# Output projection of a hybrid attention layer: residual added in mid-product, two sums of y kept in DRAM, last product by token blocks

## The chip, the cores and the metric

The kernel runs on one core of a Trainium2 chip. The metric is the device time of one execution in microseconds (us). A core has a matrix engine (TensorE, PE in the profile, with its weight loads as PEld), a vector engine (VectorE, DVE), a scalar engine (ScalarE, ACT), a general engine (GpSimd, POOL) and SyncE (SP), whose queue issues every DMA of this kernel in program order.

## What is computed

One layer over 1024 tokens of width 2048: an input projection, sliding-window attention and gated linear attention on its pieces, an output projection, and a LayerNorm over the residual sum. The change touches only the end:

```python
y = jnp.einsum('bse,ed->bsd', jnp.concatenate([y_a, y_g], axis=-1), w_out[l])
x = _layer_norm(DN_ALPHA * x + y, ln_g[l], ln_b[l])      # mean and variance over 2048 columns
```

`y` going in is 1024 x 2048, `w_out` 2048 x 2048, everything float32.

## The kernel before

Up to about 1110 us the input projection and both attention groups run; their results, the input of the output projection, are stored transposed in DRAM (`yd`, sixteen 128-row pieces for each half H of the tokens). What follows is the stretch that matters here.

**Seven products.** Token half, inner half and column half make a 2 x 2 block product, done in Winograd's form with seven half-size products instead of eight, in the order 1, 6, 7, 4, 5, 3, 2. Sums of weight blocks were stored earlier in `td`; sums of `y` blocks are made on POOL when they are needed (`y_part`, L709 to L717): one subtraction for product 7, one addition for 5, two operations for 6, three for 3. A product has two column halves `fp` of 512, four blocks `t` of 128 tokens and eight steps `k` of 128 rows. float32 is split in a rounded part and a remainder (`split`, L109: ScalarE rounds, L113; VectorE subtracts, L114), and each step takes three matmuls 128 x 512 (L740 to L742): 96 for a column half, 192 for a product, 1344 in all.

**Loops.** For six products and the first half of the seventh, `k` is the outer loop and the four token blocks the inner one, in four PSUM banks; all four are complete together. In the second half of product 2 (`last`) the token block is the outer loop, so the blocks end one after another. When a bank is complete, `collect` adds it into the output rows `pre` (eight tiles 128 x 2048; blocks 0 to 3 are the upper token half, 4 to 7 the lower). The lower half is complete after product 5, the upper one after product 2.

**Residual, statistics, norm.** For columns 0 to 1023 the residual x is loaded into `pre` itself and scaled when a product is added. For columns 1024 to 2047 `residual(tb)` (L768) loads 512 KB into a slot of the pool `raw`, adds it on VectorE (L772) and takes two statistics; it runs after the second half of product 5 (lower half) and of product 3 (upper half). `norm` (L744) then works on 608 columns with ScalarE and POOL (L751 to L757) and on 1440 with VectorE (L761, L762), in three pieces of 480 for the very last block, and stores the rows.

**Slots and queues.** `raw` has four slots of 128 x 1024; weight loads (L728, L731) and residual loads share them. `wsp` holds eight split weight pieces, `xsp` sixteen split `y` pieces (a `y` sum's operands take slots there too). A scheduler orders each engine's instructions when the kernel is built, so an instruction can stand far from its place in the text; after that every engine and SyncE's queue keep their order, and what stands behind a waiting instruction waits too.

## Time and profile before

| | |
|---|---|
| runs | 1463.07, 1466.36, 1465.85 us, median 1465.85 |
| profiled execution | 1466.27 us, of which the profile's span is 1464.4 us |
| TensorE busy | 1419.3 us (97% of the span) |
| VectorE, ScalarE, POOL busy | 886.2, 605.9, 370.4 us (61%, 41%, 25%) |
| mean granted TensorE clock | 0.987 of full speed |
| HBM read, written | 184.66 MB, 33.55 MB |

Busy time is the union of an engine's instructions. Matmuls are pipelined: one takes about 0.39 us from its start to its end but the next starts earlier, so the rate is read from starts, and a busy TensorE says only that it did not wait. Times inside the span count from its start.

### The profile page before, as it was taken

How to read it: one execution, taken by the hardware profiler on the slowest of the kernel's cores; microseconds unless marked ns; L12 is line 12 of the kernel's file. 1: busy time of each engine (PE TensorE's matmuls, PEld its weight loads, DVE VectorE, ACT ScalarE, POOL GpSimd, SP SyncE). 2: the span in 40 equal slices, each digit the busy share in tenths (PEclk: the TensorE clock that was granted, in tenths of full speed). 3: DMA queues.
4: the chain of work that ended last, by engine and by line, in shares of the span. 5: the costliest groups of instructions: out<-in, count | busy, mean ns of one | idle time of the engine just before them, and what ended most of it. 6: DMA issues, size and time to landing. Idle time of an engine off the chain costs nothing.

```text
span 1464.4 us, 23613 instructions
## 1 busy us (share of the span) xinstructions
PE 1419.3 (97%) x8992; PEld 1183.5 (81%) x8992; DVE 886.2 (61%) x1522; ACT 605.9 (41%) x1278; POOL 370.4 (25%) x373
## 2 busy tenths in 40 slices
PE   8999999999999999999999999999999999997984
PEld 5888788888888977888889888888988888885763
DVE  5566556555655665566556555655565555567968
ACT  5544345434434554444335435443553434322321
POOL 0132211212221122232211221310023231465505
PEclk9999999999999999999999999999999999998987
DMA  8243344343434346443344343433235967666642
GB/s 311 94 150 113 126 131 145 120 132 127 148 109 137 117 158 214 138 138 123 122 145 137 123 132 119 148 108 115 94 113 179 360 204 222 192 217 210 215 130 115
DMA packets 101392, 224.47 MB, mean 153 GB/s; under 512 B 11040, under 2 KB 44192, under 8 KB 101024
## 3 DMA queue, kind: packets, MB, share of 16 engines
q1 hardware_dynamic: 101280, 222.98, 46.0%
q8 instruction: 70, 1.15, 0.3%
q14 instruction: 42, 0.34, 0.1%
HBM read 184.66 MB, written 33.55 MB: 149 GB/s over the span
## 4 chain that ended last, share of the span: by engine, by line
PE 92%; DVE 5%; DMA 1%; issue 1%; POOL 1%; ACT 0%; SPq 0%; DVEq 0%; ACTq 0%
PE acc L172 17%; PE acc L174 17%; PE acc L173 17%; PE acco L740 6%; PE acco L741 6%; PE acco L742 6%; PE accv L186 4%; PE accv L188 4%; PE accv L187 4%; PE po L291 2%; PE pa L360 1%; PE ps L260 1%; PE ps L259 1%; PE pt L281 1%; PE lracc L310 1%; DVE pre L762 1%
## 5 line engine op out<-in xcount | busy, mean ns | idle before, releaser
L114 DVE TENSOR_TENSOR wl<-raw,wh 128x512 fp32r<-128x512 f32 x445 | 344.4, 781 | 270.2 <-ACT wh L113 245.6
L113 ACT CAST wh<-raw 128x512 fp32r<-128x512 f32 x445 | 272.2, 620 | 444.5 <-PE acc L173 279.6
L172 PE MATMUL acc<-xh,wh 128*128 128x512 f32 x1088 | 429.4, 396 | 6.6 <-ACT wh L113 6.6
L174 PE MATMUL acc<-xh,wl 128*128 128x512 f32 x1088 | 426.6, 392 | 0.0
L173 PE MATMUL acc<-xl,wh 128*128 128x512 f32 x1088 | 426.5, 392 | 0.0
L172 PEld LDWEIGHTS acc<-xh,wh 128*128 128x128 f32 x1088 | 204.7, 188 | 53.8 <-ACT wh L113 7.6
L174 PEld LDWEIGHTS acc<-xh,wl 128*128 128x128 f32 x1088 | 204.6, 188 | 44.7 <-issue 1.4
L173 PEld LDWEIGHTS acc<-xl,wh 128*128 128x128 f32 x1088 | 204.8, 188 | 43.0 <-issue 2.2
L740 PE MATMUL acco<-wh,xh 128*128 128x512 f32 x436 | 168.0, 395 | 14.6 <-ACT wh L113 14.6
L741 PE MATMUL acco<-wl,xh 128*128 128x512 f32 x436 | 171.8, 394 | 3.9 <-DVE wl L114 3.9
L742 PE MATMUL acco<-wh,xl 128*128 128x512 f32 x436 | 171.0, 393 | 0.0
L186 PE MATMUL accv<-wh,xh 128*128 128x256 f32 x512 | 145.3, 284 | 0.0
L188 PE MATMUL accv<-wh,xl 128*128 128x256 f32 x512 | 145.0, 283 | 0.0
L187 PE MATMUL accv<-wl,xh 128*128 128x256 f32 x512 | 144.8, 283 | 0.0
L716 POOL TENSOR_TENSOR yr<-yr 128x512 f32<-128x512 f32 x56 | 79.6, 1424 | 150.1 <-DMA yr<-yd 145.3
L740 PEld LDWEIGHTS acco<-wh,xh 128*128 128x128 f32 x436 | 82.7, 190 | 32.7 <-ACT wh L113 15.5
L741 PEld LDWEIGHTS acco<-wl,xh 128*128 128x128 f32 x436 | 82.9, 190 | 22.0 <-DVE wl L114 4.6
L186 PEld LDWEIGHTS accv<-wh,xh 128*128 128x128 f32 x512 | 98.1, 192 | 1.2 <-issue 0.7
L188 PEld LDWEIGHTS accv<-wh,xl 128*128 128x128 f32 x512 | 98.1, 192 | 0.6 <-issue 0.3
L187 PEld LDWEIGHTS accv<-wl,xh 128*128 128x128 f32 x512 | 98.2, 192 | 0.5
L742 PEld LDWEIGHTS acco<-wh,xl 128*128 128x128 f32 x436 | 83.0, 190 | 17.3
L278 POOL TENSOR_TENSOR s<-s,sm 128x512 f32<-128x512 f32 x32 | 37.2, 1163 | 214.0 <-DVE sm L277 111.5
(173 smaller groups left out, 1707.2 us busy)
## 6 DMA issues: line engine op xcount, KB each, us to landing
raw<-in_w_e_dram SPq DMA_DIRECT2D x134, 512.0 KB, 3.9
yr<-yd SPq DMA_DIRECT2D x112, 256.0 KB, 4.8
raw<-in_w_v_dram SPq DMA_DIRECT2D x32, 512.0 KB, 4.4
raw<-in_w_out_dram SPq DMA_DIRECT2D x128, 128.0 KB, 2.6
td<-raw SPq DMA_DIRECT2D x32, 512.0 KB, 3.5
raw<-td SPq DMA_DIRECT2D x32, 512.0 KB, 4.3
raw<-in_w_out_dram SPq DMA_DIRECT2D x24, 512.0 KB, 4.5
raw<-in_xT_dram SPq DMA_DIRECT2D x15, 512.0 KB, 4.7
```

Source lines behind the costliest of these rows:

```text
L113: A.copy(hi, src)
L114: V.tensor_tensor(lo, src, hi.bitcast(F32), ALU.subtract)
L172: PE.matmul(acc, wh[:, c], xh, start=(k == 0), stop=False)
L173: PE.matmul(acc, wh[:, c], xl, start=False, stop=False)
L174: PE.matmul(acc, wl[:, c], xh, start=False, stop=(k == KT - 1))
L186: PE.matmul(o, xh[:, t], wh[:, c], start=(k == 0 and tb % 2 == 0), stop=False, skip_group_check=True)
L187: PE.matmul(o, xh[:, t], wl[:, c], start=False, stop=False, skip_group_check=True)
L188: PE.matmul(o, xl[:, t], wh[:, c], start=False, stop=(k == KT - 1), skip_group_check=True)
L716: G.tensor_tensor(a, a, b, ALU.add if sign > 0 else ALU.subtract)
L740: PE.matmul(acc, yh[:, c], wh, start=(k == 0), stop=False)
L741: PE.matmul(acc, yh[:, c], wl, start=False, stop=False)
L742: PE.matmul(acc, yl[:, c], wh, start=False, stop=(k == 7))
```

## The change

Four things. The residual of columns 1024 to 2047 gets two slots of its own (`res`) in place of the six slots that `last` used, and is loaded and added at the head of products 4 (upper half) and 5 (lower half); the statistics of those columns are taken by `collect` once a column half is complete. Product 6 stores two of its sums of `y` in DRAM (`ysum`, sixteen pieces of 256 KB), and products 5 and 3 load them: product 5 makes no sum any more, product 3 one instead of three. Product 2 takes the token block as its outer loop for both column halves, with the weights of the first half in slots of `xsp`.

```diff
@@ -159,6 +159,7 @@
 
 
     td = [dr_p.tile([P, 16, 4, 256], F32, name=f"td{f}") for f in range(2)]
+    ys_d = [dr_p.tile([P, 8 * T], F32, name=f"ysum{i}") for i in range(2)]
     yd = [[dr_p.tile([P, 4 * T], F32, name=f"yd{H}_{q}") for q in range(4)] for H in range(2)]
 
 
@@ -690,7 +691,7 @@
 
     op = ctx.enter_context(tc.tile_pool(name="op", bufs=5, space=PSUM, reuse_waits="tile"))
     lp = ctx.enter_context(tc.tile_pool(name="lp", bufs=1, reuse_waits="tile"))
-    w2_p = ctx.enter_context(tc.tile_pool(name="w2", bufs=3, reuse_waits="tile"))
+    r_p = ctx.enter_context(tc.tile_pool(name="res", bufs=2, reuse_waits="tile"))
     pre = [lp.tile([P, D], F32, name=f"pre{tb}") for tb in range(2 * NB)]
     stats = [lp.tile([P, 4, 6], F32, name=f"stats{tb}") for tb in range(2 * NB)]
     gb = lp.tile([P, D], F32, name="gb")
@@ -708,15 +709,30 @@
 
     def y_part(i, k):
 
-        at = {1: "00", 2: "01", 3: "01", 4: "11", 5: "10", 6: "10", 7: "00"}[i]
-        a = y_raw(int(at[0]), int(at[1]), k, "xh")
-        more = {3: ((0, 0, 1), (1, 0, -1), (1, 1, -1)), 5: ((1, 1, 1),), 6: ((1, 1, 1), (0, 0, -1)), 7: ((1, 0, -1),)}
-        for n, (h, g, sign) in enumerate(more.get(i, ())):
-            b = y_raw(h, g, k, "xl" if n % 2 == 0 else "xh")
-            G.tensor_tensor(a, a, b, ALU.add if sign > 0 else ALU.subtract)
+        at = {1: "00", 2: "01", 3: "01", 4: "11", 6: "10", 7: "00"}
+        if i == 5:
+            a = x_p.tile([P, T], F32, name="yr", tag="xh")
+            SP.dma_start(a, ys_d[0][:, k * T:k * T + T])
+            return split(a, x_p, "x")
+        a = y_raw(int(at[i][0]), int(at[i][1]), k, "xh")
+        if i == 6:
+            b = y_raw(1, 1, k, "xl")
+            c = y_raw(0, 0, k, "xl")
+            G.tensor_tensor(a, a, b, ALU.add)
+            SP.dma_start(ys_d[0][:, k * T:k * T + T], a)
+            G.tensor_tensor(c, a, c, ALU.subtract)
+            SP.dma_start(ys_d[1][:, k * T:k * T + T], c)
+            a = c
+        elif i == 7:
+            b = y_raw(1, 0, k, "xl")
+            G.tensor_tensor(a, a, b, ALU.subtract)
+        elif i == 3:
+            b = x_p.tile([P, T], F32, name="yr", tag="xl")
+            SP.dma_start(b, ys_d[1][:, k * T:k * T + T])
+            G.tensor_tensor(a, a, b, ALU.subtract)
         return split(a, x_p, "x")
 
-    def w_parts(i, fp, pools):
+    def w_parts(i, fp, pool, tag):
 
         out = []
         for q in range(4):
@@ -730,7 +746,6 @@
                     j = {5: 0, 7: 1, 4: 2, 6: 3}[i]
                     SP.dma_start(r.rearrange("p u (h c) -> p (u h) c", h=2), td[fp][:, 4 * q:4 * q + 4, j])
             for u in range(2):
-                pool, tag = pools(2 * q + u)
                 out.append(split(r[:, u], pool, tag))
         return out
 
@@ -767,11 +782,9 @@
 
     def residual(tb):
 
-        r = raw_p.tile([P, 1024], F32, name="raw", tag="raw")
+        r = r_p.tile([P, 1024], F32, name="res", tag="res")
         SP.dma_start(r, xr[tb * P:tb * P + P, 1024:])
         V.scalar_tensor_tensor(pre[tb][:, 1024:], r, ALPHA, pre[tb][:, 1024:], ALU.mult, ALU.add)
-        for eg in (2, 3):
-            stat(tb, eg)
 
     def collect(i, fp, t, acc):
         lo, hi = slice(fp * 512, fp * 512 + 512), slice(1024 + fp * 512, 1024 + fp * 512 + 512)
@@ -790,13 +803,12 @@
         elif i == 5:
             V.tensor_tensor(c22, c22, acc, ALU.add)
             V.tensor_tensor(c12, c12, acc, ALU.add)
+            stat(NB + t, 2 + fp)
             if fp:
-                residual(NB + t)
                 norm(NB + t, False)
         elif i == 3:
             V.tensor_tensor(c12, c12, acc, ALU.add)
-            if fp:
-                residual(t)
+            stat(t, 2 + fp)
         else:
             V.tensor_tensor(c11, c11, acc, ALU.add)
             stat(t, fp)
@@ -812,25 +824,38 @@
         if i == 7:
             SP.dma_start(gb, g_d)
             SP.dma_start(bb, b_d)
+        if i in (4, 5):
+            for t in range(NB):
+                residual(t + (NB if i == 5 else 0))
+
+        def banks(n):
+            nonlocal count
+            out = []
+            for _ in range(n):
+                pool, tag = (mm, "mm") if count % 8 < 3 else (op, "op")
+                out.append(pool.tile([P, 512], F32, name="acco", tag=tag))
+                count += 1
+            return out
+
+        if i == 2:
+            ys = [y_part(i, k) for k in range(8)]
+            ws = [w_parts(i, 0, x_p, "x"), w_parts(i, 1, w_p, "w")]
+            for t in range(NB):
+                for fp, acc in enumerate(banks(2)):
+                    for k in range(8):
+                        product(acc, ys[k], ws[fp][k], t, k)
+                    collect(i, fp, t, acc)
+            continue
         ys = []
         for fp in range(2):
-            accs = []
-            for t in range(NB):
-                pool, tag = (mm, "mm") if count % 8 < 3 else (op, "op")
-                accs.append(pool.tile([P, 512], F32, name="acco", tag=tag))
-                count += 1
-            last = i == 2 and fp == 1
-            ws = w_parts(i, fp, lambda k: (w2_p, "v") if last and k > 4 else (w_p, "w"))
+            accs = banks(NB)
+            ws = w_parts(i, fp, w_p, "w")
             for k in range(8):
                 if fp == 0:
                     ys.append(y_part(i, k))
-                if not last:
-                    for t in range(NB):
-                        product(accs[t], ys[k], ws[k], t, k)
+                for t in range(NB):
+                    product(accs[t], ys[k], ws[k], t, k)
             for t in range(NB):
-                if last:
-                    for k in range(8):
-                        product(accs[t], ys[k], ws[k], t, k)
                 collect(i, fp, t, accs[t])
```

What it does to the order of the instructions is shown at three places. Names end in a number for the buffer; L numbers are lines of the kernel before in its rows and of the changed kernel in its own.

The first place is SyncE's queue between products 3 and 2. `raw<-in_xr` is the residual, `raw<-in_w_out` a weight load, `out` a store of finished rows of the lower half. Before:

```order
L771 DMA raw_13754<-in_xr_dram 128x1024
L758 DMA out_0_dram<-pre4_11399 128x608
L763 DMA out_0_dram<-pre4_11399 128x1440
L706 DMA yr_13935<-yd0_3_115 128x512
L758 DMA out_0_dram<-pre5_11400 128x608
L763 DMA out_0_dram<-pre5_11400 128x1440
L771 DMA raw_13760<-in_xr_dram 128x1024
L763 DMA out_0_dram<-pre6_11401 128x1440
L758 DMA out_0_dram<-pre6_11401 128x608
L763 DMA out_0_dram<-pre7_11402 128x1440
L758 DMA out_0_dram<-pre7_11402 128x608
L728 DMA raw_13769<-in_w_out_dram 128x1024
```

The same place after the change:

```order
L744 DMA raw_13759<-in_w_out_dram 128x1024
L744 DMA raw_13769<-in_w_out_dram 128x1024
L744 DMA raw_13779<-in_w_out_dram 128x1024
L773 DMA out_0_dram<-pre4_11401 128x608
L778 DMA out_0_dram<-pre4_11401 128x1440
L773 DMA out_0_dram<-pre5_11402 128x608
L778 DMA out_0_dram<-pre5_11402 128x1440
L744 DMA raw_13789<-in_w_out_dram 128x1024
L744 DMA raw_13799<-in_w_out_dram 128x1024
L744 DMA raw_13809<-in_w_out_dram 128x1024
L778 DMA out_0_dram<-pre6_11403 128x1440
L773 DMA out_0_dram<-pre6_11403 128x608
```

The residual's loads are gone from here, and six of product 2's eight weight loads (each brings two pieces) now stand ahead of the stores of `pre6` and `pre7`; before, the first of them stood behind all stores. The last two follow the stores of `pre7`.

The second place is VectorE around the end of product 3. L797 (L810 after) adds a bank of product 3, L772 the residual, L766 (L781) is a statistic, L114 a remainder of a split. Before:

```order
L762 SCALAR_TENSOR_TENSOR pre7_11402<-pre7_11402,rr_13323,bb_11412 128x1440
L797 TENSOR_TENSOR pre0_11395<-pre0_11395,acco_13601 128x512
L797 TENSOR_TENSOR pre1_11396<-pre1_11396,acco_13602 128x512
L772 SCALAR_TENSOR_TENSOR pre0_11395<-raw_13742,pre0_11395 128x1024
L797 TENSOR_TENSOR pre2_11397<-pre2_11397,acco_13603 128x512
L772 SCALAR_TENSOR_TENSOR pre1_11396<-raw_13748,pre1_11396 128x1024
L797 TENSOR_TENSOR pre3_11398<-pre3_11398,acco_13604 128x512
L766 BN_STATS stats0_11403<-pre0_11395 128x6 x2
L772 SCALAR_TENSOR_TENSOR pre2_11397<-raw_13754,pre2_11397 128x1024
L766 BN_STATS stats1_11404<-pre1_11396 128x6 x2
L772 SCALAR_TENSOR_TENSOR pre3_11398<-raw_13760,pre3_11398 128x1024
L114 TENSOR_TENSOR wl_13772<-raw_13769,wh_13771 128x512
```

After the change (between its L777 of `pre7` and the first row here stand seven L114):

```order
L810 TENSOR_TENSOR pre0_11397<-pre0_11397,acco_13563 128x512
L810 TENSOR_TENSOR pre1_11398<-pre1_11398,acco_13564 128x512
L781 BN_STATS stats0_11405<-pre0_11397 128x6
L810 TENSOR_TENSOR pre2_11399<-pre2_11399,acco_13565 128x512
L781 BN_STATS stats1_11406<-pre1_11398 128x6
L810 TENSOR_TENSOR pre3_11400<-pre3_11400,acco_13566 128x512
L114 TENSOR_TENSOR xl_13796<-raw_13789,xh_13795 128x512
L781 BN_STATS stats2_11407<-pre2_11399 128x6
L114 TENSOR_TENSOR wl_13822<-raw_13819,wh_13821 128x512
L114 TENSOR_TENSOR wl_13826<-raw_13819,wh_13825 128x512
L781 BN_STATS stats3_11408<-pre3_11400 128x6
L114 TENSOR_TENSOR wl_13832<-raw_13829,wh_13831 128x512
```

Before, the first remainder of product 2's weights stands behind four additions of the residual and four statistics; after, eleven of the sixteen are made ahead of product 3's last additions, four among and behind them, and the last, `wl_13836`, is the next row.

The third place is SyncE's queue in product 6, at the sixth to eighth `y` pieces (`yr` is an operand, `raw<-td` a stored weight sum). Before:

```order
L731 DMA raw_12027<-td1_111 128x4x256
L706 DMA yr_11951<-yd1_1_117 128x512
L706 DMA yr_11956<-yd0_1_113 128x512
L706 DMA yr_11953<-yd1_3_119 128x512
L731 DMA raw_12037<-td1_111 128x4x256
L731 DMA raw_12153<-td0_110 128x4x256
L731 DMA raw_12163<-td0_110 128x4x256
L706 DMA yr_11975<-yd1_1_117 128x512
```

After the change:

```order
L722 DMA ysum0_112<-yr_11939 128x512
L747 DMA raw_12055<-td1_111 128x4x256
L707 DMA yr_11965<-yd1_1_119 128x512
L707 DMA yr_11967<-yd1_3_121 128x512
L707 DMA yr_11969<-yd0_1_115 128x512
L724 DMA ysum1_113<-yr_11943 128x512
L747 DMA raw_12171<-td0_110 128x4x256
L747 DMA raw_12181<-td0_110 128x4x256
L747 DMA raw_12191<-td0_110 128x4x256
L722 DMA ysum0_112<-yr_11965 128x512
L724 DMA ysum1_113<-yr_11969 128x512
L707 DMA yr_11991<-yd1_1_119 128x512
```

The loads of a piece now stand behind the stores of the piece before, and a store waits for POOL's sum. On TensorE the last two of the eight steps of product 6's first column half begin at the product's 116th and 157th matmul, where they began at its 82nd and 112th, with matmuls of the second column half in between.

## Rows read from the trace of the kernel before

**Rows 1.** The page: span, chain by engine, a weight load's KB and us to landing.

```profile
span 1464.4 us, 23613 instructions
...
PE 92%; DVE 5%; DMA 1%; issue 1%; POOL 1%; ACT 0%; SPq 0%; DVEq 0%; ACTq 0%
...
raw<-in_w_out_dram SPq DMA_DIRECT2D x24, 512.0 KB, 4.5
```

**Rows 2.** Stretches: us, engines' busy us (instructions), granted clock, DMA share, GB/s.

```profile
1250.00:1330.00 80.00, 80.00 (x355) 66.24 (x354) 45.10 (x60) 21.31 (x36) 45.94 (x33) 1.00 0.65 209
1330.00:1350.00 20.00, 9.97 (x32) 7.24 (x31) 19.79 (x27) 6.21 (x11) 9.01 (x6) 0.74 0.59 188
1140.00:1170.00 30.00, 30.00 (x134) 24.82 (x134) 16.70 (x25) 11.04 (x21) 5.99 (x4) 1.00 1.05 387
```

**Rows 3.** Waits in the output projection: waiter <- releaser, us, times, longest.

```profile
PE acco L740 <- ACT wh L113: 14.6, 2, 8.5
...
SPq L728 <- DVE pre L772: 23.7, 8, 11.3
```

**Rows 4.** Timeline of PE: start, us, engine, line, operation, count, idle before.

```profile
1332.48 0.39 PE L742 MATMUL acco<-wh,xl 128*128 128x512 f32 x1
...
1338.98 2.08 PE L740 MATMUL acco<-wh,xh 128*128 128x512 f32 x4 [6.11 <-ACT wh L113]
...
1348.40 1.08 PE L740 MATMUL acco<-wh,xh 128*128 128x512 f32 x4
...
1388.99 0.39 PE L742 MATMUL acco<-wh,xl 128*128 128x512 f32 x1
...
1403.02 1.08 PE L740 MATMUL acco<-wh,xh 128*128 128x512 f32 x4
...
1427.34 0.40 PE L742 MATMUL acco<-vh,xl 128*128 128x512 f32 x1
...
1444.00 0.40 PE L742 MATMUL acco<-vh,xl 128*128 128x512 f32 x1
```

**Rows 5.** Groups of instructions, 1330 to 1400 us: busy, mean ns, idle before.

```profile
L772 DVE SCALAR_TENSOR_TENSOR pre<-raw,pre 128x1024 f32<-128x1024 f32 x8 | 10.8, 1354 | 0.0
L752 POOL TENSOR_TENSOR pre<-pre,gb 128x608 f32<-128x608 f32 x4 | 8.8, 2195 | 6.1 <-ACT pre L751 6.1
L757 POOL TENSOR_TENSOR pre<-pre,bb 128x608 f32<-128x608 f32 x4 | 8.5, 2134 | 4.3 <-ACT pre L756 4.3
```

**Rows 6.** Timeline of DVE.

```profile
1330.87 0.69 DVE L791 TENSOR_TENSOR pre<-pre,acco 128x512 f32<-128x512 f32 x1 [0.21 <-PE acco L742]
1331.47 0.68 DVE L792 TENSOR_TENSOR pre<-pre,acco 128x512 f32<-128x512 f32 x1
...
1346.53 0.25 DVE L747 BATCH_NORM_AGGREGATE mv<-stats 128x2 f32<-128x24 f32 x1
...
1389.13 1.27 DVE L797 TENSOR_TENSOR pre<-pre,acco 128x512 f32<-128x512 f32 x2
...
1427.78 0.69 DVE L801 TENSOR_TENSOR pre<-pre,acco 128x512 f32<-128x512 f32 x1 [2.61 <-PE acco L742]
...
1433.86 1.72 DVE L762 SCALAR_TENSOR_TENSOR pre<-pre,rr,bb 128x1440 f32<-128x1440 f32 x1
...
1448.41 0.67 DVE L801 TENSOR_TENSOR pre<-pre,acco 128x512 f32<-128x512 f32 x1
...
1457.05 3.19 DVE L762 SCALAR_TENSOR_TENSOR pre<-pre,rr,bb 128x480 f32<-128x480 f32 x3
```

**Rows 7.** Timeline of SyncE's queue at product 2, of POOL in product 6.

```profile
1391.65 13.28 SPq L728 DMA_DIRECT2D raw<-in_w_out_dram  x7
...
1179.03 2.66 POOL L716 TENSOR_TENSOR yr<-yr 128x512 f32<-128x512 f32 x2 [5.71 <-DMA yr<-yd]
```

**Rows 8.** Timeline of POOL and of DVE in product 3.

```profile
1365.65 2.06 POOL L752 TENSOR_TENSOR pre<-pre,gb 128x608 f32<-128x608 f32 x1 [3.59 <-ACT pre L751]
...
1366.29 1.98 DVE L114 TENSOR_TENSOR wl<-raw,wh 128x512 fp32r<-128x512 f32 x1
```

## Prediction, made before the changed kernel had run

> **What bounds the kernel now.** I read first the page: a span of 1464.4 us, in which the chain that ended last is TensorE for 92% [rows 1]. TensorE therefore sets the time wherever it never waits, and what can be won lies where it does. The table of stretches gives the place: from 1250 to 1330 us TensorE is busy for 80.00 of 80.00 us at a granted clock of 1.00, while VectorE is busy for only 45.10 us; from 1330 to 1350 TensorE is busy for 9.97 of 20, its granted clock is 0.74 in the mean, and VectorE is full with 19.79 [rows 2]. Ahead of 1330 there is nothing to win, behind it there is.
>
> The list of waits names what ends them: TensorE waits 14.6 us in 2 waits for a weight piece rounded by ScalarE (L113), and SyncE's queue, ahead of loads of `w_out` (L728), waits 23.7 us in 8 for the residual's addition L772 on VectorE [rows 3]. The chain is then: the residual's load sits in one of the four `raw` slots, the slot comes free when VectorE has done the addition, only then does SyncE issue the next weight load, and ScalarE, VectorE and TensorE follow. One hole lies in front of product 3, the other in front of product 2.
>
> TensorE's own rows give the sizes. Product 5's last matmul starts at 1332.48, and full rate is back at 1348.40; in between 13 matmuls start (that one, four L740, and eight of L741 and L742). Product 3's last starts at 1388.99, and full rate is back at 1403.02, again with 13 [rows 4]. From 1348.40 to 1388.99 lie 179 starts, 0.2268 us each. The last matmul of all starts at 1444.00, 20.40 us ahead of the end.
>
> **The sum, part by part,** against the profiled execution (span 1464.4 us; its own time is 1466.27 us, 1.87 us more, and lies 0.42 us above the median of the runs, 1465.85).
>
> (a) *Residual from slots of its own, in products 4 and 5.* Eight loads and eight additions move; none is added. SyncE no longer holds a weight load behind an addition, and the stage in front of product 3 becomes like the boundary of products 4 and 5 near 1289 us, which lies in the 80 us without a gap [rows 2]. The hole is worth 1348.40 - 1332.48 = 15.92 us less 13 x 0.2268 = 2.95: **-13.0 us**. The eight additions, 10.8 us [rows 5], now lie in the time before 1330 us, where VectorE had 80.00 - 45.10 = 34.9 us idle; I cost them at nothing there. Were that cover gone, TensorE would wait for up to those 10.8 us. The 16 statistics stay; four of them, for columns 1024 to 1535 of the lower half, are now done in the middle of product 5.
>
> (b) *Hole in front of product 2.* By the order, six of its eight weight loads are now issued ahead of the last stores of `out`, and no addition stands in front: 1403.02 - 1388.99 = 14.03 us less 2.95: **-11.1 us**, if nothing takes its place. Something does: see (d).
>
> (c) *Last product one token block at a time.* Now the last four blocks of 24 matmuls follow each other faster than VectorE can normalize. The first block's L801 starts 0.44 us after its last matmul (1427.34 to 1427.78), the last one's 4.41 us after (1444.00 to 1448.41) [rows 4, 6]. With 48 matmuls a block takes 48 x 0.2268 = 10.9 us, and VectorE needs 7.80 us for a block (1427.78 to the end of L762 at 1435.58) plus an addition and a statistic for the other column half, 2 x 0.68, which is 9.2 us: it keeps up. Then the end is 0.44 + 7.80 + 4.16 us, the last being from the end of L762 to the end of the span (1457.05 + 3.19 = 1460.24 to 1464.4), and some 1.0 us for the last block's norm in three pieces (bounds: 0, and twice what the triple of L762 takes more than the one piece today, 2 x (3.19 - 1.72) = 2.9): 13.4 instead of 20.4 us, **-7.0 us** (between -8.0 and -5.1).
>
> (d) *What becomes late instead.* Product 2 now needs all eight `y` pieces and all sixteen weight pieces within its first 10.9 us, and VectorE makes the remainders. Today it runs without a gap from the first BN_AGGR of the lower half's norms (1346.53) to product 3's second round of L797 (1389.13), 42.6 us [rows 6]. Counted in the order, the same stretch after the change holds the same work: 31 operations 512 wide (21 remainders, 6 statistics, 4 additions, where there were 23, 4, 4) and the four norms. What moves is its start: 13 operations follow product 5's first L791 at 1330.87, at 0.60 us each by the next start (1331.47), so 1338.7. VectorE is thus at L797 at 1338.7 + 42.6 = 1381.3. Product 3 without holes starts its last matmul at 1332.48 + 192 x 0.2268 = 1376.0, so matmul m of product 2 is due at 1376.3 + 0.2268 m. In the order the last remainder of column half 0 is the 7th operation from L797, ready at 1381.3 + 7 x 0.6 = 1385.5, and is needed by matmul 32, at 1383.6; the last of half 1 is the 13th, ready at 1389.1, needed by matmul 49, at 1387.4. TensorE waits **+2 us**. The clock fell today after an idle stretch of 6.11 us [rows 4]; a wait of 2 us has no row, so I take no loss for it; the bound is 12 matmuls at half rate, 2.7 us. Loads: today they leave from 1391.65 on [rows 7], behind the stores of `out`, which follow VectorE's last L762 of the lower half just ahead of L797. After the change this L762 comes seven remainders ahead of L797, near 1377, so the last two loads leave near 1379 and 1381 and land 4.5 us later [rows 1], in time for the 9th and the 12th operation.
>
> (e) *Two sums kept in DRAM.* 32 of POOL's 56 additions of `y` pieces (L716) go. No wait of TensorE hangs on them today, since products 5 and 3 get their pieces ahead of time: 0. By the code 24 loads of `yr` go, and 16 stores of 256 KB come into product 6, behind POOL in SyncE's queue. There the transfers are full today: 387 GB/s from 1140 to 1170 [rows 2]. From the first `pre` load to the last `yr` load of product 6 the order has 13568 KB before and 16640 KB after (six stores, two residual loads, one more `td`), 3.15 MB or 8.1 us more. The sum for the last piece ends today at 1181.69 [rows 7], so 1189.8, split by 1191.2; TensorE's order now uses that piece from matmul 157 of product 6, not 112. Product 6 starts at 1332.48 - 767 x 0.2268 = 1158.5, so it is needed at 1194.1. 2.9 us are left: **0**.
>
> Sum: 1464.4 - 13.0 - 11.1 - 7.0 + 2.0 = 1435.3; with the 1.87 us around the span, **1437 us**, 29 us (2.0%) below the profiled execution.
>
> **The rivals.** *A: VectorE is later than its measured stretch.* POOL's eight 608-wide operations of the norms take 8.8 + 8.5 = 17.3 us in that stretch [rows 5]. At 0.60 us for each of the 31 operations, 1.72 for each of the eight L761 and L762 and an estimated 2.3 for the small ones, it would need 34.7 us, so 7.9 of its 42.6 us are delay. One is seen: a remainder at 1366.29 ends at 1368.27, 0.56 us after POOL's L752 ended at 1367.71 [rows 8]. If VectorE stood still for all 17.3, it would be 9.4 us later: 1446 us. Against it: the same eight operations lay beside the same work today. The Trainium skill, SBUF — State Buffer, Who interferes with whom, says that a VectorE operation with two SBUF inputs and a GpSimd operation that reads SBUF exclude each other for a whole instruction; the row at 1366.29 agrees, and by that rule at its worst the sum would be rival A's.
>
> *B: product 6 starves.* The 3 us of (e) rest on one rate of transfer. Three loads wait behind a store that waits for the POOL sum of the piece before; if each of the last two pieces is 5 us later than counted, TensorE stops for up to 10 - 2.9 = 7.1 us, plus some 2.7 us at half rate: 1440 to 1447 us.
>
> *C: slower, by the clock.* If VectorE's lateness reaches TensorE in small waits all through products 3 and 2, the granted clock could stay at the lower level, as from 1338.98 to 1348.40 [rows 4]. All 384 matmuls at 1.2 GHz cost 384 x 0.2 = 77 us: 1514 us. It is slower than before from some 145 matmuls on (29 us / 0.2). Against it: between the holes TensorE kept its 0.2268 us beside a VectorE without a gap [rows 4, 6].
>
> *D: the hole in front of product 2 stays.* If the weight loads came as late as today (seven issued over 13.28 us from 1391.65 [rows 7]), the first block, which now needs all of them, would wait some 12 us more than the hole does now: 1460 us. The order speaks against it: three loads stand ahead of all those stores, six ahead of the last four.
>
> **How the numbers follow.** Chances: forecast 0.70 (1434 to 1443), A 0.10, B 0.13, D 0.04, C 0.03. The low end is no wait at all and the shortest end (1437 - 2 - 1). The high end takes in A and B with some 3 us for both in part: 1434 to 1450. A measurement of this kernel can tell 0.2%, 3 us, from no change. Every case but C and a worse D is faster: faster 0.95, same 0.02, slower 0.03.
>
> **What would show it.** In the changed profile: no residual addition on SyncE's list of waits ahead of `w_out` loads; TensorE full with a clock of 1.00 through the start of product 3; a wait of about 2 us near 1383 to 1389 us on a remainder of VectorE; 13 to 14 us between the last matmul and the end; no TensorE wait in product 6. I am wrong if TensorE waits over 6 us at the start of product 2, or at all before 1330 us.

## The result, and the profile after

The changed kernel takes **1453.51 us** (median of 4 runs, 1451.04 to 1454.69) against 1465.88 of the kernel before on the same chip: a ratio of 0.9917, 95% interval 0.9899 to 0.9936. That is 12 us faster, where 29 us were forecast, and outside the range of 1434 to 1450. The profiled execution took 1452.95 us, with a span of 1451.1.

The stretches of the changed kernel (columns as in [rows 2]):

```profile
1120.00:1145.00 25.00, 21.27 (x100) 16.72 (x99) 9.12 (x21) 6.83 (x15) 8.82 (x8) 0.93 0.60 187
1205.00:1225.00 20.00, 17.89 (x72) 14.31 (x71) 12.73 (x20) 6.80 (x13) 5.12 (x4) 0.91 0.54 178
1250.00:1330.00 80.00, 80.00 (x354) 66.24 (x353) 65.30 (x88) 26.81 (x47) 25.23 (x16) 1.00 0.72 229
1330.00:1350.00 20.00, 20.00 (x90) 16.57 (x89) 13.62 (x23) 7.38 (x13) 0.99 (x1) 1.00 0.57 173
1385.00:1405.00 20.00, 14.83 (x56) 10.84 (x55) 20.00 (x30) 8.14 (x14) 5.51 (x2) 0.91 0.62 217
```

The first two of these stretches in the kernel before:

```profile
1120.00:1145.00 25.00, 25.00 (x124) 20.19 (x123) 12.80 (x25) 9.16 (x18) 11.65 (x10) 1.00 0.69 217
1205.00:1225.00 20.00, 20.00 (x90) 16.57 (x89) 11.04 (x18) 7.80 (x14) 4.10 (x3) 1.00 0.57 177
```

The hole of [rows 2] is gone: TensorE is busy for 20.00 of 20 us from 1330 to 1350. VectorE made the eight additions ahead of it, and TensorE did not wait for them (from 1250 to 1330 VectorE is busy for 65.30 us in place of 45.10, TensorE for 80.00 of 80). But TensorE now stops in two stretches where it was full before, near 1131 and 1213 us, and longer than forecast near 1390. The waits (as in [rows 3]) name three different releasers:

```profile
PE acco L755 <- ACT xh L113: 3.8, 2, 2.1
PE po L472 <- DVE on L441: 3.7, 1, 3.7
PE acco L756 <- DVE xl L114: 3.4, 2, 3.2
```

TensorE's timeline (as in [rows 4]; L755 to L757 are the lines that were L740 to L742, L472 transposes the attention's output):

```profile
1131.41 0.39 PE L757 MATMUL acco<-wh,xl 128*128 128x512 f32 x1
1135.53 1.20 PE L472 MATMUL po<-cst,on 128*128 128x128 f32 x4 [3.73 <-DVE on L441]
...
1138.95 0.39 PE L755 MATMUL acco<-wh,xh 128*128 128x512 f32 x1
...
1213.55 0.39 PE L757 MATMUL acco<-wh,xl 128*128 128x512 f32 x1
1216.05 0.50 PE L755 MATMUL acco<-wh,xh 128*128 128x512 f32 x1 [2.11 <-ACT xh L113]
...
1220.95 0.40 PE L756 MATMUL acco<-wl,xh 128*128 128x512 f32 x1
...
1386.44 0.39 PE L755 MATMUL acco<-xh 128*128 128x512 f32 x1
...
1388.93 0.39 PE L757 MATMUL acco<-xh,xl 128*128 128x512 f32 x1
1390.98 0.50 PE L755 MATMUL acco<-xh 128*128 128x512 f32 x1 [1.66 <-ACT xh L113]
1394.71 0.77 PE L756 MATMUL acco<-xl,xh 128*128 128x512 f32 x1 [3.23 <-DVE xl L114]
...
1437.47 0.39 PE L757 MATMUL acco<-wh,xl 128*128 128x512 f32 x1
```

Each hole is worth its length less the work in it, at 0.2268 us from one matmul's start to the next. The first: 1138.95 - 1131.41 = 7.54 us, less 7 matmuls (1.59) and the four transposes (0.35 us where they meet no wait, from 1118.99 to 1119.34), 5.6 us. The second: 1220.95 - 1213.55 = 7.40, less 15 matmuls (3.40), 4.0 us. Product 2 begins at 1386.44 instead of the forecast 1376.2; 10.2 = 5.6 + 4.0 and some 0.6 that this execution has lost before 1131. From the first matmul of product 2 to the last pass 51.03 us; 191 starts of 0.2268 need 43.32: 7.7 us are lost there. The tail is 1451.1 - 1437.47 = 13.6 us.

Why TensorE stops at 1131 is seen in SyncE's list of waits, where the first of the two stores of a piece waits for POOL's sum, and in the rows of SyncE's queue, POOL and VectorE:

```profile
SPq L722 <- POOL yr L721: 22.6, 6, 6.0
```

The rows:

```profile
1116.53 1.37 SPq L707 DMA_DIRECT2D yr<-yd  x3
1122.38 0.32 SPq L722 DMA_DIRECT2D ysum<-yr  x1
1123.74 0.32 SPq L724 DMA_DIRECT2D ysum<-yr  x1
1124.11 1.40 SPq L707 DMA_DIRECT2D yr<-yd  x3
...
1130.31 1.29 POOL L721 TENSOR_TENSOR yr<-yr 128x512 f32<-128x512 f32 x1 [6.59 <-DMA yr<-yd]
1131.67 1.26 POOL L723 TENSOR_TENSOR yr<-yr 128x512 f32<-128x512 f32 x1
1132.89 0.70 POOL L455 TENSOR_TENSOR rr<-rv,mhalf 128x2 f32<-128x2 f32 x1
...
1127.11 0.17 DVE L454 TENSOR_SCALAR rv<-ss 128x2 f32<-128x2 f32 x1 [0.36 <-ACT on L438]
1133.63 0.16 DVE L456 TENSOR_TENSOR rt<-rr 128x2 f32<-128x2 f32 x1 [6.35 <-POOL rr L455]
```

The three loads of a piece of product 6 stand on SyncE behind the two stores of the piece before, which wait for POOL's sums of that piece. So a new round begins only when the last has ended: loads at 1116.53, stores from 1122.38, loads again at 1124.11. POOL in turn works in order: L455, a step of the attention's last normalization whose input is ready at 1127.28, stands behind L721 and L723, which wait for those loads until 1130.31. VectorE waits 6.35 us for it, and TensorE's transposes behind that. The transposes that wait here started at 1130.94 in the kernel before, without a wait.

The later pieces are late too: the sums for product 6's last piece end at 1195.75, where the forecast had 1189.8, and product 7's third piece is not there at 1213.55. Its second load stands on SyncE behind the load of a stored weight sum, which waits from 1201.87 to 1209.55 for a `raw` slot:

```profile
1209.55 0.37 SPq L747 DMA_DIRECT2D raw<-td  x1
1209.97 0.98 SPq L707 DMA_DIRECT2D yr<-yd  x2
```

Each stop is followed by some matmuls at the lower of the two clock levels, 0.43 us from start to start (granted clock 0.93 and 0.91 in the two stretches).

VectorE's rows at products 3 and 2 (as in [rows 6]; L804 was L791, L762 was L747, L810 was L797):

```profile
1344.62 0.69 DVE L114 TENSOR_TENSOR xl<-yr,xh 128x512 fp32r<-128x512 f32 x1 [3.51 <-ACT xh L113]
...
1346.61 0.68 DVE L804 TENSOR_TENSOR pre<-pre,acco 128x512 f32<-128x512 f32 x1
...
1354.38 0.26 DVE L762 BATCH_NORM_AGGREGATE mv<-stats 128x2 f32<-128x24 f32 x1
...
1396.99 1.27 DVE L810 TENSOR_TENSOR pre<-pre,acco 128x512 f32<-128x512 f32 x2
```

From the first L762 to the second round of L810 it takes 1396.99 - 1354.38 = 42.6 us, the length of the forecast. But it starts 15.7 us after the forecast 1338.7, 5.5 more than TensorE's 10.2: VectorE stood idle for 6.3 us in three waits, the last of them 3.51 us, for product 2's `y` pieces, whose remainders stand ahead of product 5's last additions in its order.

### The profile page after: what moved, and what is told of

Its sections match the earlier page's. It is cut to its first block, busy times and chain, and to the rows that moved or that the text cites. A ratio compares the mean times of both kernels' runs of the same rounds, so it can differ in the third digit from the quotient of the medians.

```text
span 1451.1 us, 23545 instructions
## 1 busy us (share of the span) xinstructions
PE 1420.2 (98%) x8992; PEld 1184.2 (82%) x8992; DVE 881.7 (61%) x1522; ACT 605.5 (42%) x1278; POOL 336.7 (23%) x349
## 5 line engine op out<-in xcount | busy, mean ns | idle before, releaser
L114 DVE TENSOR_TENSOR wl<-raw,wh 128x512 fp32r<-128x512 f32 x440 | 334.3, 766 | 283.2 <-ACT wh L113 259.2
L113 ACT CAST wh<-raw 128x512 fp32r<-128x512 f32 x440 | 268.9, 620 | 422.2 <-PE acc L174 279.0
L755 PE MATMUL acco<-wh,xh 128*128 128x512 f32 x416 | 162.0, 392 | 2.1 <-ACT xh L113 2.1
L756 PE MATMUL acco<-wl,xh 128*128 128x512 f32 x416 | 162.8, 391 | 0.0
L757 PE MATMUL acco<-wh,xl 128*128 128x512 f32 x416 | 162.0, 392 | 0.0
L755 PEld LDWEIGHTS acco<-wh,xh 128*128 128x128 f32 x416 | 78.9, 190 | 18.8 <-ACT xh L113 2.5
L757 PEld LDWEIGHTS acco<-wh,xl 128*128 128x128 f32 x416 | 78.9, 190 | 16.6
L756 PEld LDWEIGHTS acco<-wl,xh 128*128 128x128 f32 x416 | 78.5, 189 | 16.3
L113 ACT CAST xh<-yr 128x512 fp32r<-128x512 f32 x56 | 34.6, 621 | 119.7 <-POOL yr L732 30.8
```

The source lines that it names most:

```text
L113: A.copy(hi, src)
L114: V.tensor_tensor(lo, src, hi.bitcast(F32), ALU.subtract)
L755: PE.matmul(acc, yh[:, c], wh, start=(k == 0), stop=False)
L756: PE.matmul(acc, yh[:, c], wl, start=False, stop=False)
L757: PE.matmul(acc, yl[:, c], wh, start=False, stop=(k == 7))
```

## The experiments

The times are medians; the last three columns are read from the profiled execution of each run. "Late" is when product 2's first matmul starts; "lost" is what TensorE loses from there to its last matmul (the rule above); "tail" is from that one to the end. In e1, e3 and e10 product 2's first matmul itself waits, for 4.35, 7.94 and 4.97 us; that time is in "late" and not in "lost".

| run | us | ratio, 95% interval | late | lost | tail |
|---|---|---|---|---|---|
| after | 1453.5 | 0.9917 (0.9899 to 0.9936) | 1386.44 | 7.7 | 13.6 |
| e1_no_sums | 1461.0 | 0.9959 (0.9945 to 0.9973) | 1400.71 | 7.5 | 13.7 |
| e3_last_alone | 1462.2 | 0.9974 (0.9964 to 0.9983) | 1398.38 | 5.3 | 13.7 |
| e4_sums_alone | 1475.1 | 1.0061 (1.0046 to 1.0076) | | | 20.4 |
| e6_act_stores | 1445.3 | 0.9862 (0.9847 to 0.9876) | 1376.92 | 9.9 | 13.6 |
| e7_more_slots | 1448.0 | 0.9875 (0.986 to 0.989) | 1378.45 | 11.9 | 13.7 |
| e8_late_norms | 1449.2 | 0.9882 (0.9867 to 0.9897) | 1376.12 | 2.4 | 25.1 |
| e10_residual_back | 1459.9 | 0.9956 (0.9942 to 0.997) | 1394.85 | 8.3 | 13.7 |
| e11_slots_norms | 1447.9 | 0.9875 (0.9861 to 0.9890) | 1375.92 | 0.6 | 25.1 |
| e12_norms_vector | 1436.6 | 0.9809 (0.9794 to 0.9823) | 1376.66 | 1.1 | 13.7 |
| e13_one_late | 1445.7 | 0.9873 (0.9858 to 0.9887) | 1376.07 | 10.2 | 14.1 |
| e14_both | 1437.4 | 0.9815 (0.98 to 0.983) | 1376.20 | 4.2 | 13.7 |
| e15_y2_pool | 1445.2 | 0.9866 (0.9849 to 0.9882) | 1376.62 | 10.2 | 13.9 |
| e16_y2_slots | 1443.0 | 0.9844 (0.9829 to 0.9859) | 1376.83 | 7.6 | 13.7 |
| e17_vector_slots | 1435.2 | 0.9787 (0.9771 to 0.9803) | 1376.71 | 0.0 | 13.6 |

### Which part costs: the sums

**e4_sums_alone**: the kernel before, with the change's `y_part` and `ys_d`.

> The kernel before with the two sums in DRAM alone. Theory S: the same two waits as in the changed kernel, near 1131 us (TensorE waits for the attention's L441) and near 1213 us (a y piece of product 7), 9.5 us in all: 1466 + 9.5 = 1475 us. Rival T: no such waits, 1466 us. A third: fewer POOL sums in product 3 let its pieces come early enough to shorten the hole in front of it, by up to 5 us: 1470 us.

Measured 1475.1 us, 9 us slower. The first wait is there, in this run's list of waits:

```profile
PE po L472 <- DVE on L441: 4.3, 1, 4.3
```

A `y` piece of product 7 is late here too, twice, for 1.9 us in all, and TensorE loses 3.0 us in product 7. Neither the residual nor the last product is needed for this.

**e6_act_stores**: the same stores from ScalarE's queue.

```
-            SP.dma_start(ys_d[0][:, k * T:k * T + T], a)
+            A.dma_start(ys_d[0][:, k * T:k * T + T], a)
...
-            SP.dma_start(ys_d[1][:, k * T:k * T + T], c)
+            A.dma_start(ys_d[1][:, k * T:k * T + T], c)
```

> The changed kernel with the sixteen stores of the sums issued from ScalarE's queue instead of SyncE's: the same bytes, the same POOL operations, but the loads of the next piece no longer stand behind a store that waits for POOL. If the order on SyncE is the cause (theory S), the two waits near 1131 and 1213 us are gone or under 2 us together: 1444 to 1446 us. If the 4 MB of stores themselves are (DMA engines full, rival U), they stay: 1453 us. A cost of its own may come in, ScalarE's casts behind a store that waits for POOL; each has at most the 1.3 us of one POOL sum.

Measured 1445.3 us. Its stretches:

```profile
1120.00:1145.00 25.00, 25.00 (x124) 20.16 (x123) 14.94 (x25) 9.57 (x19) 11.83 (x10) 1.00 0.82 273
1205.00:1225.00 20.00, 20.00 (x89) 16.11 (x87) 7.03 (x11) 5.91 (x11) 5.28 (x4) 1.00 0.67 210
...
1376.00:1400.00 24.00, 17.44 (x63) 12.59 (x62) 23.93 (x39) 9.32 (x17) 5.49 (x2) 0.86 0.61 195
```

TensorE is full in both stretches, though the kernel moves the same bytes (in the first stretch even more of them, 273 GB/s in place of 187); 1.1 us are still lost in product 7, behind these stretches. POOL's order is the same in both kernels, so that the lateness at 1131 came from the loads' place on SyncE, and POOL only handed it on. The Trainium skill, DMA: Bandwidth & Descriptors, Issuing engines are not separate DMA queues, says that issuing from several engines saves only the sequencer's time to initiate the transfers, usually small. Here that would be 16 x 0.32 = 5.1 us at most, an estimate from the rows above; the run gained 8.2, since an issue that waits holds back the loads behind it, and the measurement decides.

**e1_no_sums**: the changed kernel with the `y_part` of before and without `ys_d`.

```
-        if i == 5:
-            a = x_p.tile([P, T], F32, name="yr", tag="xh")
-            SP.dma_start(a, ys_d[0][:, k * T:k * T + T])
...
+        more = {3: ((0, 0, 1), (1, 0, -1), (1, 1, -1)), 5: ((1, 1, 1),), 6: ((1, 1, 1), (0, 0, -1)), 7: ((1, 0, -1),)}
...
```

> The changed kernel without the two sums in DRAM: the y pieces of products 6, 5 and 3 are added up on POOL as before, the residual's own slots and the last product's order stay. Theory S (the sums cost 9.5 us: their stores stand on SyncE between the loads of product 6, and POOL, waiting for those loads, holds back the attention's last L455 and product 7's pieces): no TensorE wait ahead of product 3, 1453.5 - 9.5 = 1444 us if the wait at the start of product 2 stays as it is, down to 1438.5 if that goes back to the predicted 2 us. Rival T (the waits near 1131 and 1213 us come from the transfers of the residual and of the other pieces, not from the sums): 1453 us, and the two waits stay.

Measured 1461.0 us (the profiled execution, from which the rows come, took 1467.0, 6 us more). I was wrong twice. The stop near 1131 is gone, as theory S has it, but the one in product 7 is not:

```profile
1217.24 0.50 PE L739 MATMUL acco<-wh,xh 128*128 128x512 f32 x1 [1.98 <-ACT xh L113]
```

With a second wait of 0.90 us it costs 3.6 us, against 4.0 in the changed kernel, and no sum is stored here. So this stop comes with the sums alone (e4, 3.0 us) and with the rest of the change alone, and only the stop near 1131 is the stores' alone; what in the rest brings it is not shown. And TensorE now waits four times in product 3, for 10.7 us, and twice at product 2's start; ScalarE waits 15.4 us for POOL's sums of product 3's pieces. With the residual out of the way, product 3 needs its pieces earlier than four loads and three sums each can bring them. So keeping the sums does carry part of the gain; what costs, near 1131 at least, is how they are stored.

### The residual and the last product

**e10_residual_back**: e6 with `residual` and `collect` of before, without `r_p`.

```
             if fp:
+                residual(NB + t)
                 norm(NB + t, False)
         elif i == 3:
             V.tensor_tensor(c12, c12, acc, ALU.add)
-            stat(t, 2 + fp)
+            if fp:
+                residual(t)
...
-        if i in (4, 5):
-            for t in range(NB):
-                residual(t + (NB if i == 5 else 0))
```

> The run with ScalarE's stores (1445 us), with the residual put back: loaded into the raw slots and added behind products 5 and 3, as before the change. If term (a) is right, the hole in front of product 3 is back, 13 us, and the wait in front of product 2 grows by some 5 us, since its weight loads stand behind the second four additions: 1463 us. Rival Q (it was the sum read from DRAM, one load in place of three, that closed the hole, and the residual's place is worth nothing): 1445 to 1447 us.

Measured 1459.9 us. Product 3's last matmul starts at 1389.49 here and at 1376.69 in e6: 12.8 us for the hole that (a) put at 13.0. SyncE again waits 18.8 us in 8 for the addition. Rival Q falls. From product 3's last matmul to the end of product 2 TensorE loses 13.4 us, 3.5 more than in e6, where 5 more were expected.

**e3_last_alone**: the kernel before with the new end loop, `w_parts` and `banks`, without `w2_p`.

```
+        if i == 2:
+            ys = [y_part(i, k) for k in range(8)]
+            ws = [w_parts(i, 0, x_p, "x"), w_parts(i, 1, w_p, "w")]
+            for t in range(NB):
+                for fp, acc in enumerate(banks(2)):
...
```

> The kernel before with the last product's order alone (one token block at a time, its weights of column half 0 in slots of the y pieces); the residual stays in the raw slots and no sum is kept. If the tail is the whole of it: 1466 - 7 = 1459 us, 13.5 us from the last matmul to the end. If product 2's first block, which needs all sixteen weight pieces, now waits behind the residual's additions: the hole in front of product 2 grows from 11 to some 18 to 23 us and eats the gain: 1465 to 1471 us. I take the second. The hole in front of product 3 stays at 13 us in both.

Measured 1462.2 us, between the two. The tail is 13.7 us; of the 6.7 us that it gives, 2.0 are lost again around product 2's start (13.4 us in place of 11.5, the longest wait 7.9 us for a rounded piece), and 1.1 ahead of it.

### What is lost at the start of product 2

In e6 TensorE is on time, and loses 9.9 us there. VectorE in e6:

```profile
1339.13 0.68 DVE L804 TENSOR_TENSOR pre<-pre,acco 128x512 f32<-128x512 f32 x1
...
1346.91 0.26 DVE L762 BATCH_NORM_AGGREGATE mv<-stats 128x2 f32<-128x24 f32 x1
...
1354.23 1.47 DVE L456 TENSOR_TENSOR rt<-rr 128x1 f32<-128x1 f32 x1
...
1389.50 1.27 DVE L810 TENSOR_TENSOR pre<-pre,acco 128x512 f32<-128x512 f32 x2
```

and POOL there:

```profile
1352.35 3.33 POOL L767 TENSOR_TENSOR pre<-pre,gb 128x608 f32<-128x608 f32 x1
```

Again 42.6 us from L762 to L810, but from 1346.91, 8.2 us after the forecast. The forecast 2.0 and these 8.2 are 10.2; measured are 9.9.

**e7_more_slots**: `w_parts` takes every second piece from the residual's slots.

```
-            r = raw_p.tile([P, 2, 512], F32, name="raw", tag="raw")
+            own = q % 2 and (i == 2 or i == 3 and fp)
+            r = (r_p if own else raw_p).tile([P, 2, 512], F32, name="raw", tag="res" if own else "raw")
```

> The run with ScalarE's stores (1445 us), and every second weight load of product 3's column half 1 and of product 2 goes into the residual's two slots, which are free by then: six slots instead of four. Theory V: the 7 us that TensorE still waits at the start of product 2 come from VectorE's start; it stands idle for 5.5 us in 3 waits near 1329 to 1337 us for y pieces of product 2, whose loads stand on SyncE behind weight loads that wait for a raw slot. With two more slots these waits shrink to under 2 us, and the time falls by 3 to 5 us: 1440 to 1442. Rival P: VectorE's 42.6 us run between the norms and the second round of product 3's additions is what is too long (POOL beside it), whenever it starts: the y pieces come earlier and nothing changes, 1445.

Measured 1448.0 us; VectorE's three waits stay (5.7 us). Weight slots are not what the pieces wait for. The run is 2.8 us slower than e6: product 2 loses 11.9 us in place of 9.9, and TensorE waits 1.7 us in product 3; the cause is open.

**e15_y2_pool** (e6): `y_raw` issues product 2's loads from POOL's queue.

```
...
-        a = y_raw(int(at[i][0]), int(at[i][1]), k, "xh")
+        a = y_raw(int(at[i][0]), int(at[i][1]), k, "xh", G if i == 2 else SP)
```

> The run with ScalarE's stores (1445 us), with the eight loads of product 2's y pieces issued from POOL's queue, so that they no longer stand on SyncE between weight loads that wait for raw slots. If SyncE's order is why VectorE stands idle for 5.5 us near 1329 to 1337 us, these three waits are gone and the time falls by 4 to 5 us: 1440 to 1441 us. If the y pieces wait for something else (their slots, which TensorE frees): 1445 us.

Measured 1445.2 us, no change, but POOL's rows name the wait:

```profile
1329.96 0.55 POOL L707 DMA_DIRECT2D yr<-yd  x1 [4.96 <-DVE xl L114]
```

A load waits for a remainder of an earlier piece, which frees the slot.

**e16_y2_slots** (e6) and **e17_vector_slots** (e12, below): product 2's pieces get slots to land in.

```
+    q_p = ctx.enter_context(tc.tile_pool(name="yq", bufs=3, reuse_waits="tile"))
...
+        a = y_raw(int(at[i][0]), int(at[i][1]), k, *(("yq", q_p) if i == 2 else ("xh",)))
```

> The run with ScalarE's stores (1445 us), with product 2's y pieces loaded into three slots of their own, from which ScalarE and VectorE split them into the old slots; queue and order stay. In the run with POOL's queue the loads waited for the remainder of the piece before, that is for the slot it was loaded into. If that is why VectorE stands idle for 5.5 us ahead of product 5's last additions, the three waits go, VectorE's run starts up to 5.5 us earlier, and of the 9.9 us that TensorE loses in product 2 some 4.4 are left: 1440 us. If the pieces wait for the slots of the split values, which TensorE frees, nothing changes: 1445 us.

Measured 1443.0 us: VectorE's run starts 3.2 us earlier (1343.74), TensorE loses 7.6 instead of 9.9. The slots are part of it. VectorE's first addition of product 5's end still comes at 1335.96, not 1330.87: three waits of 3.3 us in all are left ahead of it, the longest, 2.26 us, put down to TensorE, and the rest is order, remainders for the next two products that stand in front.

**e8_late_norms**, **e13_one_late**, **e11_slots_norms**: `norm(NB + t, False)` moved from `collect` into product 2's loop, ahead of each block (e8, e11 with e7's slots), or for the last block alone behind the first (e13). In e8:

```
-            if fp:
-                norm(NB + t, False)
...
             for t in range(NB):
+                norm(NB + t, False)
```

> The run with ScalarE's stores (1445 us), and the norms of the lower half stand in the program one ahead of each token block of product 2 instead of behind product 5: by the order the first stays ahead of product 2, the other three come into it. If VectorE's work ahead of product 2 is the bound (theory V), 3 x 3.4 us of it go from there and TensorE's 7 us wait at the start of product 2 is under 1 us; but VectorE had only some 5 us idle in product 2, so that part of it comes back behind the last matmul, whose 13.6 us grow by 2 to 6: 1440 to 1445 us. Rival R (the weight loads of product 2, on SyncE behind stores of the lower half, are the bound): the wait at the start stays above 5 us, and the time is 1445 or more.

> The run with ScalarE's stores (1445 us), with one of the four norms of the lower half (the last block's) moved behind the first token block of product 2. Some 5 us of VectorE's work go from in front of product 2, and VectorE had about that idle inside it. If VectorE's amount of work in the two stretches is the bound, the 7 us wait at the start of product 2 falls to some 2 us and the end behind the last matmul stays at 13.6 us: 1440 us. If the weight loads are the bound: 1445 us.

> Both together: six slots for the last weight loads and the three norms of the lower half moved into product 2. By theory V the wait at the start of product 2 is gone and VectorE starts 3 to 5 us earlier, so that less of the moved work is left behind the last matmul: 1436 to 1441 us, the fastest of all. By P or R 1445.

Measured 1449.2, 1445.7 and 1447.9 us. In e11 TensorE does not wait over 0.4 us and is done at 1419.88, 17.6 us earlier than in the changed kernel, but the end is 25.1 us away: VectorE's work has only moved behind the last matmul, whose tail grows by 11.5 us where 2 to 6 were expected. Rival R does not hold in e8, where the longest wait is 1.5 us; but in e13 the start still costs 10.2 us, and TensorE's longest wait, 5.0 us, is for a piece whose weight load left late, behind stores of `out`. In none of the three does moving VectorE's work gain anything; the next run makes it less.

**e12_norms_vector**: the lower half's norms without POOL and ScalarE.

```
+        if tb >= NB:
+            return norm_v(tb)
...
+        V.scalar_tensor_tensor(z, z, mv[:, 0:1], gb, ALU.subtract, ALU.mult)
+        V.scalar_tensor_tensor(z, z, rs, bb, ALU.mult, ALU.add)
+        SP.dma_start(out[tb * P:tb * P + P], z)
```

> The run with ScalarE's stores (1445 us), and the four norms of the lower half are done by VectorE alone over all 2048 columns; ScalarE's and POOL's shares of 608 columns are gone there. Theory P: POOL holds VectorE up in the 42.6 us ahead of product 2; seven operations there take 8.9 us more than their like elsewhere (128x1 operations 1.45 instead of 0.15 us, remainders 1.95 instead of 0.68, one L777 2.94 instead of 1.71). Without POOL these go, and 8 x 608 columns come in, 8 x 0.72 = 5.8 us: 3 us shorter, 1442 us. Rival: POOL is not what lengthens them, and the 5.8 us are simply added: 1451 us.

Measured 1436.6 us, 8.6 less than e6, where 3 were expected. VectorE's groups from the first L762 to the second round of L810, in e6:

```profile
L114 DVE TENSOR_TENSOR wl<-raw,wh 128x512 fp32r<-128x512 f32 x13 | 11.2, 872 | 0.0
L777 DVE SCALAR_TENSOR_TENSOR pre<-pre,rr,bb 128x1440 f32<-128x1440 f32 x4 | 8.0, 2012 | 0.0
...
L456 DVE TENSOR_TENSOR rt<-rr 128x1 f32<-128x1 f32 x4 | 3.2, 798 | 0.0
L459 DVE TENSOR_TENSOR rr<-rr,rt 128x1 f32<-128x1 f32 x4 | 3.0, 770 | 0.0
```

and in e12 (its L788 was L777):

```profile
L788 DVE SCALAR_TENSOR_TENSOR pre<-pre,rr,bb 128x2048 f32<-128x2048 f32 x4 | 9.2, 2342 | 0.0
L114 DVE TENSOR_TENSOR wl<-raw,wh 128x512 fp32r<-128x512 f32 x9 | 6.1, 679 | 0.0
...
L456 DVE TENSOR_TENSOR rt<-rr 128x1 f32<-128x1 f32 x4 | 0.6, 142 | 0.4 <-POOL rr L455 0.4
L459 DVE TENSOR_TENSOR rr<-rr,rt 128x1 f32<-128x1 f32 x4 | 0.5, 152 | 0.0
```

The mean remainder of a weight piece falls from 872 to 679 ns, these two 128x1 steps from some 780 to 147, and 2048 columns cost VectorE 2.34 us where 1440 took 1.71 to 2.92. Fewer delays give 8.7 us, the columns take 8 x 0.63 = 5.1, and four remainders (4 x 0.60 = 2.4 us) are not in this stretch any more: 36.8 us instead of 42.6. ScalarE's share of the norms went together with POOL's; that POOL is what lengthens these operations rests on the rows, where L456 of e6 and POOL's L767 end within 0.02 us of each other (1355.70 and 1355.68). TensorE's only wait in the output projection is then 0.64 us, and the granted clock from 1376 to 1400 is 1.00, where it was 0.86 in e6.

> Both: the norms of the lower half on VectorE alone, and the last of them behind product 2's first block. If both theories hold, 1445 - 3 - 5 = 1437 us, and TensorE waits less than 2 us in all at the start of product 2.

**e14_both** (e12 and e13's edit) took 1437.4 us, no better than e12; the time is the one expected, but all of it comes from e12's part.

> The run with the lower half's norms on VectorE alone (1436.6 us, TensorE loses 1.1 us in product 2), with the three slots for product 2's y pieces. At most that 1.1 us is left to win there: 1435.5 to 1437 us. If the time falls by more, the loss in product 2 is not what bounds it any more.

**e17_vector_slots** took 1435.2 us, the fastest, 2.1% below the kernel before and 1.3% below the change (by the ratios, 0.9787 / 0.9917). TensorE has no wait left in the output projection:

```profile
1120.00:1145.00 25.00, 25.00 (x124) 20.20 (x123) 15.17 (x25) 9.57 (x19) 11.69 (x10) 1.00 0.80 258
1205.00:1225.00 20.00, 20.00 (x90) 16.57 (x89) 9.17 (x13) 7.06 (x12) 5.58 (x4) 1.00 0.70 216
...
1376.00:1400.00 24.00, 24.00 (x107) 19.88 (x106) 20.21 (x35) 6.38 (x12) 3.42 (x2) 1.00 0.36 137
```

## Why the prediction was right or wrong

- **(a), right in size, but not by the residual alone.** TensorE is full through product 3's start; putting the residual back costs 12.8 us there, against 13.0. The eight additions cost nothing where they went. What the sum did not say is that both parts are needed: between product 5's last matmul and product 3's last TensorE loses 13.0 us in the kernel before, 12.8 with the sums alone (e4), 15.9 with the residual moved and no sums kept (e1, in its profiled execution), and 0.1 with both (e6).
- **(b), right that the old hole goes**; what took its place was sized in (d).
- **(c), right.** 13.6 us from the last matmul to the end, against 13.4, and 13.7 with this part alone (e3).
- **(d), mis-sized: 2.0 forecast, 7.7 measured** (9.9 where TensorE is on time). The failing step is "13 operations follow product 5's first L791 at 1330.87", which took VectorE to be there as early as before. The order had remainders of product 2's `y` pieces ahead of it, whose loads wait in part for slots (e15, e16); VectorE reached it 8.3 us later (e6), and the last two weight loads left 7.5 us after the forecast (e6: 1386.59 and 1388.39). The 42.6 us behind it came out to a tenth, partly by luck: POOL's delays fell on other operations than before (in the changed kernel the mean remainder of a weight piece took 871 ns in place of 1077, and L456, which was L455, 796 in place of 148).
- **(e), wrong: 0 forecast, 9.6 us measured.** This is the step that failed most. It priced the added transfers at the full rate and asked only whether product 6's last piece comes in time. That piece came 6 us later than counted (1195.75, not 1189.8) and no wait followed in product 6, since TensorE was by then as late itself. What the step left out is what stands behind a store that waits: the loads of the next piece on SyncE, and behind POOL's sums the attention's L455, for which TensorE stopped for 5.6 us. That stop comes with the sums (e4) and is gone without them (e1) and with the stores on another queue (e6). The other 4.0 us, in product 7, are not the stores' alone: 3.0 with the sums alone (e4), 3.6 without them (e1), 1.1 with the stores on ScalarE's queue (e6). The sentence that no wait of TensorE hangs on the additions that go held for the kernel before, and no longer once the residual was out of the way: without the kept sums product 3 waits for them (e1).
- **The sum** with the measured terms: 1437 + 9.6 (e) + 5.7 (d) + 0.6 = 1452.9 us; the profiled execution took 1452.95.
- **Rivals.** B had the mechanism, stores that hold back loads, but put it at product 6's last pieces with up to 7 us of waits; TensorE stopped at the attention's end and in product 7. My own test, no wait before 1330 us, failed. A was real, though not new: POOL's delays lay inside the 42.6 us (8.7 us by the rows, where the forecast had 7.9), and taking the norms off POOL and ScalarE gained 8.6 us (e12). C: the clock fell to 0.91 to 0.93 in the stretches around the stops and came back each time; in e1 a stop of nearly the second's length (2.37 us from start to start, 2.50 here) was followed by no slow matmul. D did not happen.
- **The range** left some 3 us above rival A's or B's time for both in part; (d) and (e) came together, 15.3 us above the sum.

## What to carry to other kernels

When a store is added to a queue that also issues loads, ask what it waits for and which loads stand behind it; the bytes may cost little and the wait much, and another engine's queue can take it. An operation's start is not given by the engine that feeds it alone: read what stands ahead of it in its own engine's order, and which slots those wait for. Where an engine is full in a stretch, moving its work may only move the wait; look for what lengthens its operations. Two parts of a change can need each other, as the residual's place and the kept sums did here: try each alone before giving one of them the gain.

## What the runs showed of the hardware

VectorE operations on 128x1 tiles with two inputs, which take 0.14 us with POOL idle (L456 in e6 at 1374.75), took up to 1.47 us beside POOL: L456 in e6 runs from 1354.23 to 1355.70, and POOL's L767 from 1352.35 to 1355.68, itself 3.33 us long where 1.49 is seen elsewhere (product 2). So a split of 608 of 2048 columns to POOL, meant to relieve VectorE, cost it more (8.7 us in four norms) than the columns did (5.1). The Trainium skill, SBUF — State Buffer, Who interferes with whom, says that an operation of VectorE with two SBUF inputs contends with one of GpSimd that reads SBUF, and that the shared ports are an exclusive lock; these rows and e12 agree, down to operations of one column.
